# A hybrid diffusion block on one core: the sums of the later modulations as GpSimd products and additions in place of fused VectorE instructions

## The chip, the cores and the metric

The kernel runs on one core of a Trainium2 chip. The core has five engines with a queue of instructions each: TensorE (PE in the profile; PEld is its loading of weights), VectorE (DVE), ScalarE (ACT), GpSimd (POOL) and SyncE (SP). An engine takes its instructions in order; engines wait for one another by semaphores. Transfers between the memory of the chip and the core's own memory (SBUF) are issued from the queues of SyncE, ScalarE or GpSimd and done by 16 DMA engines. The metric is the device time of one execution in microseconds (us), the median of several runs.

## The reference, cut to what matters

One layer: the tokens x (256 x 2048) and a context (256 x 2048) are modulated by a condition c, pass one wide projection into three token mixers, are merged, projected and normed, and pass a squared-ReLU MLP.

```python
mod = jax.nn.silu(c) @ w_ada[l] + b_ada[l]                    # 2048 x 12288
sh1, sc1, g1, sh2, sc2, g2 = [m[:, None, :] for m in jnp.split(mod, 6, axis=-1)]
y, _ = _token_mixers(_modulate(x, sh1, sc1), lp, ctx_states, True, True)
x = _layernorm(ALPHA * x + g1 * y, ln1_g[l], ln1_b[l])
x = _layernorm(ALPHA * x + g2 * _sq_relu_mlp(_modulate(x, sh2, sc2), w_ff1[l], w_ff2[l]),
               ln2_g[l], ln2_b[l])
```

The first two modulations (sh1, sc1) are needed at once and are computed by TensorE at the start. The change concerns the product silu(c) @ w_ada for the four later ones, g1, sh2, sc2 and g2: 2048 x 8192 weights, 67 MB of float32.

## The kernel before

Every weight matrix is streamed in tiles of 512 KB (128 partitions x 1024 float32). `wload` (line 162) gets one: `wsplit` has SyncE load it into a buffer `wraw`, ScalarE casts it to a rounded part `whi` (line 138), and VectorE subtracts the two into the rest `wlo` (line 139); TensorE multiplies with both parts. There are 4 buffers with the tag `wraw`, 4 `whi` and 3 `wlo`, and 584 such tiles go through in the whole program.

The later modulations run beside that stream. `ada_parts` (line 546) is a generator; it takes 8 parts of 1024 columns, each in 16 steps. A step has one tile `aw` (128 rows of w_ada, 512 KB), multiplies each partition with its value of silu(c) (`csil`) and adds it to `acc`, in one fused instruction on VectorE, `stt` of line 564 (line 562 for the first step of a part). A step loads the tile for the next step first. At the end of a part `acc` goes to `acc_d` in the chip's memory; much later `ada_row` and `ada_cols` read it and sum over the partitions on TensorE.

`beside` (line 152) enters a generator with a rate: each `wload` moves it on by that many steps. The six first parts (g1, sh2, sc2) run at a rate of 1.0 in `dn_early` (the projections for the DeltaNet branch, 24 tiles, with the Hyena filters between them), at 0.55 in `hyena`, at 0 in `hgrn_group`, and at 0.3 in the tail of the DeltaNet branch and the branch projections (some 1060 to 1450 us). Their tiles `aw` take buffers of the tag `wraw`, the same four that the weight stream uses. The last two parts (g2) run in the MLP at 0.25 from `first_norm`, after it has scaled and shifted the residual; they have a ring of eight buffers of their own (`awr`), and there `in_turn` keeps loads and VectorE's sums in the order of the program.

Elsewhere the order on each engine is set when the program is built: a scheduler plays it through on a clock of its own and gives each instruction its place, each buffer its user, and so each wait its semaphore. `dma` (line 131) is GpSimd's queue: the program's many small transfers (filter windows, `v_d`, `g_d`, `br_d`, `acc_d`) are issued there, and little else runs on GpSimd.

Of the kernel before, what the change touches and what calls it, by code (L numbers as in the profile page):

```python
# [14 lines left out]
MUL, ADD, SUB, MAX, MIN = ALU.mult, ALU.add, ALU.subtract, ALU.max, ALU.min  # L15
# [65 lines left out]
def tile_block(ctx: ExitStack, tc: tile.TileContext, A: dict, out: bass.AP):  # L81
    nc = tc.nc
# [9 lines left out]
    def slot(shape, tag, name, dt=F32):  # L92
        uid[0] += 1
        return sbp.tile(shape, dt, name=f"{name}_{uid[0]}", tag=tag, bufs=NB[tag])
# [32 lines left out]
    ts_ = nc.vector.tensor_scalar  # L127
    stt = nc.vector.scalar_tensor_tensor
# [71 lines left out]
    csil = cst.tile([P, 2, KT], F32, name="csil")  # L200
# [112 lines left out]
    ring = slot([P, 4, 1024], "m16", "ring", F32R)  # L313
# [62 lines left out]
    for q in range(4):  # L376
        xt = page("xt", (4, 512))
        for i, src in enumerate((x_in, c_in)):
            nc.scalar.dma_start(
                out=xt[:, 2 * i:2 * i + 2, :],  # L380
                in_=src[:, q * 512:(q + 1) * 512].rearrange("(t p) c -> p t c", p=P))
        mod = slot([P, 2, 4, 2], "k1", "mod")
        for part in range(2):
            pmod = sc_ps()
            for kb in range(8):
# [3 lines left out]
                for k in range(2):  # L389
                    kt = kb * 2 + k  # L390
# [153 lines left out]
    in_turn = tc.keep_in_program_order  # L544

    def ada_parts(parts, ring=None):
        def load(b, kt):
            a = slot([P, W], "wraw", "aw") if ring is None else ring[:, (b * KT + kt) % 8]
            ld = nc.sync.dma_start(out=a, in_=w_ada[kt * P:(kt + 1) * P, 2 * D + b * W:2 * D + (b + 1) * W])
            if ring is not None:  # L550
                in_turn(ld)
            return a

        for b in parts:
            acc = slot([P, W], "k4", "acc")
            ahead = None
            for kt in range(KT):
                a = ahead if kt else load(b, kt)
                if kt < KT - 1:
                    ahead = load(b, kt + 1)  # L560
                if kt == 0:
                    op = ts_(out=acc, in0=a, scalar1=csil[:, 0, kt:kt + 1], scalar2=None, op0=MUL)
                else:
                    op = stt(out=acc, in0=a, scalar=csil[:, 0, kt:kt + 1], in1=acc, op0=MUL, op1=ADD)  # L564
                if ring is not None:
                    in_turn(op)
                if kt == KT - 1:
                    dma(out=acc_d[b], in_=acc)
                yield
# [222 lines left out]
    def dn_inverse():  # L792
# [31 lines left out]
        dma(out=dx[1], in_=M[64:P])  # L824

    beside("ada", ada_parts(range(6)), 1.0)
    dn_early()

# [641 lines left out]
    for i, pp in tm_last(ya, yb, A["w_out"][0], 0, 3 * 512, boxes):  # L1470
# [4 lines left out]
        for k4 in range(4):  # L1475
# [9 lines left out]
            for k in range(4):  # L1485
                kt = 4 * k4 + k
                if k % 2:
                    ts_(out=t[:, k, :], in0=pt[:, k * P:(k + 1) * P], scalar1=gm[:, kt:kt + 1],
                        scalar2=bm[:, kt:kt + 1], op0=MUL, op1=ADD)
# [5 lines left out]
    def first_norm():  # L1495

        for j in range(4):
            js = slice(j * 512, (j + 1) * 512)
            gr = row_bcast(A["ln1_g"][0][js], 512, "k2", "lng")
            br = row_bcast(A["ln1_b"][0][js], 512, "k2", "lnb")  # L1500
            for i in range(2):
                in_turn(tt_(out=xr[:, i, js], in0=xr[:, i, js], in1=gr, op=MUL))
                tt_(out=xr[:, i, js], in0=xr[:, i, js], in1=br, op=ADD)
                yield
        yield from ada_parts((6, 7), slot([P, 8, W], "u32", "awr"))
# [85 lines left out]
```

## Time and profile before

| | before |
|---|---|
| runs (us) | 2358.07, 2356.26, 2362.41; median 2358.07 |
| profiled execution (us) | 2355.76, of which span 2354.1 |
| TensorE busy | 2271.1 us, 96% of the span |
| VectorE busy | 1634.0 us, 69% |
| ScalarE busy | 1081.7 us, 46% |
| GpSimd busy | 181.7 us, 8% |
| moved by DMA | 511.19 MB, 217 GB/s over the span |

The profile shows one execution. Its rows give, for a group of instructions, the line of the kernel, the engine, the output and inputs by the program's names, the count, the busy time, and the idle time before them with what ended it. A row of waits says how long an engine stood still for what. A row of the windows gives the busy time of each engine in a stretch, with the granted clock of TensorE (1.00 is full) and the share of time in which the DMA engines were busy.

### The profile page before, as it was taken

The numbers are of one execution on the slowest core, as the hardware profiler recorded it, in microseconds if no ns is written. First come the engines' busy times: TensorE is split into PE (matmuls) and PEld (weight loads), VectorE is DVE, ScalarE is ACT, GpSimd is POOL, SyncE is SP. The second block draws the span as 40 slices with busy tenths as digits, with TensorE's granted clock in tenths as the row PEclk, the third lists the DMA queues.
The fourth block names the chain that finished last, engine by engine and source line by source line (L and its number), as shares of the span: only waits on it lengthen the run. The fifth ranks groups of instructions, "written<-read, shape, count | busy, mean of one in ns | idle before, by whom it ended". The sixth has DMA issues, their size and how long they took to land.

```text
span 2354.1 us, 32778 instructions
## 1 busy us (share of the span) xinstructions
PE 2271.1 (96%) x12641; PEld 1936.4 (82%) x12641; DVE 1634.0 (69%) x1972; ACT 1081.7 (46%) x1473; POOL 181.7 (8%) x293
## 2 busy tenths in 40 slices
PE   6999898999999999999999999999999999999998
PEld 4778688998888889887888877887888888888886
DVE  6776457877879999576666656666765766765667
ACT  6665434434433534644443443445544544544542
POOL 0000222000110000111030020000000000000000
PEclk9999899999999999999999999999999999999999
DMA  9958767787653323678787898664677777776664
GB/s 344 338 183 259 219 181 229 230 261 246 206 149 110 101 73 117 173 196 275 233 251 219 287 326 280 220 208 146 214 232 245 231 246 242 232 245 193 195 204 147
DMA packets 296072, 511.19 MB, mean 217 GB/s; under 512 B 17526, under 2 KB 155217, under 8 KB 293324
## 3 DMA queue, kind: packets, MB, share of 16 engines
q1 hardware_dynamic: 271488, 422.63, 56.2%
q0 software_dynamic: 21648, 82.01, 11.2%
q10 hardware_dynamic: 2780, 4.47, 0.5%
q8 instruction: 99, 1.62, 0.3%
q14 instruction: 57, 0.47, 0.1%
HBM read 474.59 MB, written 34.45 MB: 216 GB/s over the span
## 4 chain that ended last, share of the span: by engine, by line
PE 68%; DMA 7%; DVE 5%; issue 1%; ACT 1%; DVEq 0%; POOL 0%; ACTq 0%; SPq 0%
PE mm L476 10%; PE mm L519 7%; PE mm L518 7%; PE mm L520 7%; PE mm L478 5%; PE mm L846 4%; PE mm L847 3%; PE mm L845 3%; DMA aw<-in_w_ada_dram 3%; PE mm L219 3%; PE mm L218 3%; PE mm L220 3%; DVE wlo L139 2%; DMA wraw<-in_w_in_dram 2%; DMA wraw<-in_w_branch_dram 2%
## 5 line engine op out<-in xcount | busy, mean ns | idle before, releaser
L138 ACT CAST whi<-wraw 128x1024 fp32r<-128x1024 f32 x584 | 614.0, 1052 | 898.3 <-PE mm L520 226.3
L139 DVE TENSOR_TENSOR wlo<-wraw,whi 128x1024 fp32r<-128x1024 f32 x584 | 712.0, 1221 | 391.0 <-PE mm L519 127.5
L476 PE MATMUL mm<-u,whi 128*128 128x512 f32 x992 | 349.2, 397 | 0.0
L220 PE MATMUL mm<-uh,wlo 128*128 128x256 f32 (+1 forms) x1024 | 341.1, 336 | 2.9 <-DVE wlo L139 2.9
L218 PE MATMUL mm<-uh,whi 128*128 128x256 f32 (+1 forms) x960 | 319.0, 332 | 14.1 <-DVE cy L534 13.0
L219 PE MATMUL mm<-ul,whi 128*128 128x256 f32 (+1 forms) x960 | 318.9, 332 | 0.0
L478 PE MATMUL mm<-u,wlo 128*128 128x256 f32 x992 | 278.4, 281 | 0.0
L476 PEld LDWEIGHTS mm<-u,whi 128*128 128x128 f32 x992 | 186.2, 188 | 45.2
L220 PEld LDWEIGHTS mm<-uh,wlo 128*128 128x128 f32 x1024 | 198.9, 194 | 22.9 <-DVE wlo L139 3.7
L218 PEld LDWEIGHTS mm<-uh,whi 128*128 128x128 f32 x960 | 186.7, 194 | 31.7 <-issue 13.6
L219 PEld LDWEIGHTS mm<-ul,whi 128*128 128x128 f32 x960 | 186.9, 195 | 16.0 <-issue 0.7
L478 PEld LDWEIGHTS mm<-u,wlo 128*128 128x128 f32 x992 | 187.4, 189 | 0.1
L520 PE MATMUL mm<-whi,h 128*128 128x512 f32 x480 | 187.2, 390 | 0.0
L519 PE MATMUL mm<-wlo,h 128*128 128x512 f32 x480 | 186.8, 389 | 0.0
L518 PE MATMUL mm<-whi,h 128*128 128x512 f32 x480 | 186.0, 391 | 0.0
L564 DVE SCALAR_TENSOR_TENSOR acc<-aw,csil,acc 128x1024 f32<-128x1024 f32 x90 | 115.1, 1279 | 99.0 <-DMA aw<-in_w_ada_dram 98.8
L846 PE MATMUL mm<-wlo,uh 128*128 128x512 f32 x384 | 151.0, 393 | 2.4 <-DVE wlo L139 2.4
L847 PE MATMUL mm<-whi,ul 128*128 128x512 f32 x384 | 150.9, 393 | 0.0
L845 PE MATMUL mm<-whi,uh 128*128 128x512 f32 x384 | 150.5, 400 | 0.0
L518 PEld LDWEIGHTS mm<-whi,h 128*128 128x128 f32 x480 | 90.1, 188 | 19.4 <-issue 0.7
L520 PEld LDWEIGHTS mm<-whi,h 128*128 128x128 f32 x480 | 90.1, 188 | 19.0 <-issue 0.2
L519 PEld LDWEIGHTS mm<-wlo,h 128*128 128x128 f32 x480 | 90.1, 188 | 19.0 <-issue 0.5
(515 smaller groups left out, 3977.5 us busy)
## 6 DMA issues: line engine op xcount, KB each, us to landing
wraw<-in_w_in_dram SPq DMA_DIRECT2D x264, 512.0 KB, 4.1
wraw<-in_w_ff_dram SPq DMA_DIRECT2D x256, 512.0 KB, 4.0
aw<-in_w_ada_dram SPq DMA_DIRECT2D x96, 512.0 KB, 4.6
raw<-in_w_ada_dram SPq DMA_DIRECT2D x32, 1024.0 KB, 5.5
wraw<-in_w_branch_dram SPq DMA_DIRECT2D x48, 512.0 KB, 5.2
wraw<-in_w_out_dram SPq DMA_DIRECT2D x32, 512.0 KB, 4.3
awr<-in_w_ada_dram SPq DMA_DIRECT2D x32, 512.0 KB, 5.8
g_d<-gate POOLq DMA_DIRECT2D x24, 256.0 KB, 4.0
```

The costliest lines, as they stand in the source:

```text
L138: copy(out=hi, in_=src)
L139: tt_(out=lo, in0=src, in1=hi.bitcast(F32), op=SUB)
L218: mm(ps, wh[:, k, cs], ah, start=first, stop=False, skip_group_check=True)
L219: mm(ps, wh[:, k, cs], al, start=False, stop=False, skip_group_check=True)
L220: mm(ps, wl[:, k, cs], ah, start=False, stop=last, skip_group_check=True)
L476: mm(pss[ch], wh[:, k, cs], a[:, kt].rearrange("p s t -> p (s t)"), start=(kt == 0), stop=False, skip_group_check=True)
L478: mm(pss[ch][:, 0:T], wl[:, k, cs], a[:, kt, 0], start=False, stop=(kt == KT - 1), skip_group_check=True)
L518: mm(pss[i], a, wh[:, k, :], start=(kt == 0), stop=False)
L519: mm(pss[i], a, wl[:, k, :], start=False, stop=False)
L520: mm(pss[i], b, wh[:, k, :], start=False, stop=(kt == nk - 1))
L846: mm(pg[i], a, wl[:, k, :], start=False, stop=False)
L847: mm(pg[i], c, wh[:, k, :], start=False, stop=(kt == KT - 1))
```

## The change

In `ada_parts` the fused multiply-and-add leaves VectorE. On GpSimd, a step multiplies the tile in place (`aw` by `csil`) and then adds it to `acc`, two instructions; the first step of a part is one product into `acc`. The call that held the sums of the last two parts in program order is gone; that for their loads stays. The 128 steps, the loads and the rates stay.

```diff
                 if kt == 0:
-                    op = ts_(out=acc, in0=a, scalar1=csil[:, 0, kt:kt + 1], scalar2=None, op0=MUL)
+                    op = nc.gpsimd.tensor_scalar(out=acc, in0=a, scalar1=csil[:, 0, kt:kt + 1], scalar2=None, op0=MUL)
                 else:
-                    op = stt(out=acc, in0=a, scalar=csil[:, 0, kt:kt + 1], in1=acc, op0=MUL, op1=ADD)
-                if ring is not None:
-                    in_turn(op)
+                    op = nc.gpsimd.tensor_scalar(out=a, in0=a, scalar1=csil[:, 0, kt:kt + 1], scalar2=None, op0=MUL)
+                    nc.gpsimd.tensor_tensor(out=acc, in0=acc, in1=a, op=ADD)
                 if kt == KT - 1:
                     dma(out=acc_d[b], in_=acc)
```

The instructions as they are built now, at three places. In the new file lines 562 and 564 are the products and 565 the addition; numbers behind are smaller by one. First SyncE in `dn_early`, where loads of `aw` and of weight tiles take turns; what a load waits for stands in brackets, a semaphore by its owner (DVE and Pool the engines, DMAHW a transfer). Before:

```order
L549 DMA aw_1854<-in_w_ada_dram 128x1024 [waits DMAHW2_49,DVE_49]
L143 DMA wraw_1857<-in_w_in_dram 128x4x256 [waits DMAHW3_49,DVE_49]
L549 DMA aw_1887<-in_w_ada_dram 128x1024 [waits DMAHW4_49,DVE_49]
L143 DMA wraw_1890<-in_w_in_dram 128x4x256 [waits DMAHW5_49,DVE_49]
L549 DMA aw_1920<-in_w_ada_dram 128x1024 [waits DMAHW6_49,DVE_49]
L143 DMA wraw_1923<-in_w_in_dram 128x4x256 [waits DMAHW7_49,DVE_49]
```

And now:

```order
L549 DMA aw_1861<-in_w_ada_dram 128x1024 [waits DMAHW6_49,DMAHW5_49,DVE_49]
L143 DMA wraw_1865<-in_w_in_dram 128x4x256 [waits Pool_49]
L549 DMA aw_1895<-in_w_ada_dram 128x1024 [waits DMAHW7_49,DMAHW0_49,DVE_49]
L143 DMA wraw_1899<-in_w_in_dram 128x4x256 [waits Pool_49]
L549 DMA aw_1929<-in_w_ada_dram 128x1024 [waits DMAHW2_49,DMAHW1_49,DVE_49]
L143 DMA wraw_1933<-in_w_in_dram 128x4x256 [waits Pool_49]
```

The loads stand in the same order; before, each waited for VectorE to be done with a buffer, and now every weight tile here waits for an instruction of GpSimd.

Second, VectorE at the same place, where the gates of the DeltaNet branch (`gates`) are computed in a chain of small instructions. Before:

```order
L139 TENSOR_TENSOR wlo_1860<-wraw_1857,whi_1859 128x1024
L644 SCALAR_TENSOR_TENSOR gates_1279<-gates_1279 128x64
L564 SCALAR_TENSOR_TENSOR acc_1487<-aw_1887,csil,acc_1487 128x1024
L531 SCALAR_TENSOR_TENSOR cy_1627<-mm_1486,colC,cy_1627 128x4x63
L644 SCALAR_TENSOR_TENSOR gates_1279<-gates_1279 128x64
L530 SCALAR_TENSOR_TENSOR cy_1765<-mm_1632,colC,cy_1765 128x4x63
L139 TENSOR_TENSOR wlo_1893<-wraw_1890,whi_1892 128x1024
L564 SCALAR_TENSOR_TENSOR acc_1487<-aw_1920,csil,acc_1487 128x1024
L644 SCALAR_TENSOR_TENSOR gates_1279<-gates_1279 128x64
L531 SCALAR_TENSOR_TENSOR cy_1765<-mm_1632,colC,cy_1765 128x4x63
L139 TENSOR_TENSOR wlo_1926<-wraw_1923,whi_1925 128x1024
L564 SCALAR_TENSOR_TENSOR acc_1487<-aw_1953,csil,acc_1487 128x1024
```

And now:

```order
L139 TENSOR_TENSOR wlo_1598<-wraw_1595,whi_1597 128x1024
L641 TENSOR_SCALAR gates_1279<-gates_1279 128x64
L644 TENSOR_SCALAR gates_1279<-gates_1279 128x64
L643 SCALAR_TENSOR_TENSOR gates_1279<-gates_1279 128x64 x7
L645 SCALAR_TENSOR_TENSOR gates_1279<-gates_1279 128x64
L646 SCALAR_TENSOR_TENSOR gates_1279<-gates_1279 128x64
L647 SCALAR_TENSOR_TENSOR gates_1279<-gates_1279,alg_1276 128x64
L652 COPY G<-gates_1279 128x32 x2
L139 TENSOR_TENSOR wlo_1643<-wraw_1640,whi_1642 128x1024
L530 SCALAR_TENSOR_TENSOR cy_1625<-mm_1486,colC,cy_1625 128x4x63
L531 SCALAR_TENSOR_TENSOR cy_1625<-mm_1486,colC,cy_1625 128x4x63
```

The sums (line 564) stood between the links of the chain and are gone; the chain now stands together, ahead of the next weight tile's subtraction.

Third, GpSimd in `hyena`, where it had only issued transfers (to the loads of the filters' spectra, `spl`, and the stores of the gates, `g_d`). Before:

```order
L909 DMA spl_3869<-spec_90 128x2048
L300 DMA spec_93<-smdf_2973 512x1x256
L852 DMA g_d<-gate_4091 128x512
L852 DMA g_d<-gate_4094 128x512
L909 DMA spl_4131<-spec_92 128x2048
L911 DMA nyl_4133<-nyq_96 1x16x32
L568 DMA acc_d<-acc_3596 128x1024
```

And now:

```order
L564 TENSOR_SCALAR aw_3943<-aw_3943,csil 128x1024
L564 TENSOR_SCALAR aw_4012<-aw_4012,csil 128x1024
L565 TENSOR_TENSOR acc_3626<-acc_3626,aw_3943 128x1024
L564 TENSOR_SCALAR aw_4067<-aw_4067,csil 128x1024
L565 TENSOR_TENSOR acc_3626<-acc_3626,aw_4012 128x1024
L564 TENSOR_SCALAR aw_4089<-aw_4089,csil 128x1024
L565 TENSOR_TENSOR acc_3626<-acc_3626,aw_4067 128x1024
L564 TENSOR_SCALAR aw_4191<-aw_4191,csil 128x1024
L565 TENSOR_TENSOR acc_3626<-acc_3626,aw_4089 128x1024
L851 DMA g_d<-gate_4129 128x512
L910 DMA nyl_4171<-nyq_96 1x16x32
L908 DMA spl_4169<-spec_92 128x2048
L851 DMA g_d<-gate_4132 128x512
```

The products (564) and additions (565) stand between the transfers, and the addition of a step comes behind the product of the next one, which needs the next tile.

## Rows read from the trace of the kernel before

**Rows 1.** The page: span, engines, the cast behind each weight tile, two kinds of loads.

```profile
span 2354.1 us, 32778 instructions
...
PE 2271.1 (96%) x12641; PEld 1936.4 (82%) x12641; DVE 1634.0 (69%) x1972; ACT 1081.7 (46%) x1473; POOL 181.7 (8%) x293
...
L138 ACT CAST whi<-wraw 128x1024 fp32r<-128x1024 f32 x584 | 614.0, 1052 | 898.3 <-PE mm L520 226.3
...
wraw<-in_w_in_dram SPq DMA_DIRECT2D x264, 512.0 KB, 4.1
...
aw<-in_w_ada_dram SPq DMA_DIRECT2D x96, 512.0 KB, 4.6
```

**Rows 2.** Busy time of each engine in five stretches (us; instructions in brackets).

```profile
core 0: us, PE busy (x) PEld busy (x) DVE busy (x) ACT busy (x) POOL busy (x), PEclk, DMA share, GB/s
150.00:206.00 56.00, 51.79 (x313) 46.41 (x312) 45.46 (x76) 29.21 (x40) 1.16 (x3) 0.97 0.83 257
206.00:330.00 124.00, 112.41 (x568) 93.44 (x567) 61.92 (x111) 59.95 (x136) 26.50 (x41) 0.94 0.66 202
330.00:606.00 276.00, 262.14 (x1781) 242.85 (x1780) 206.63 (x266) 118.16 (x153) 30.20 (x50) 0.98 0.76 239
1060.00:1450.00 390.00, 381.63 (x1940) 314.42 (x1938) 241.42 (x265) 164.90 (x236) 54.11 (x92) 0.99 0.81 266
1753.00:2088.00 335.00, 335.00 (x1706) 284.44 (x1705) 221.34 (x225) 156.93 (x191) 0.59 (x2) 1.00 0.72 236
```

**Rows 3.** The same stretches, instructions of line 564 alone.

```profile
150.00:206.00 56.00, 16.62 (x13) 0.97 0.83 257
206.00:330.00 124.00, 15.53 (x13) 0.94 0.66 202
...
1060.00:1450.00 390.00, 37.38 (x30) 0.99 0.81 266
1753.00:2088.00 335.00, 38.35 (x30) 1.00 0.72 236
```

**Rows 4.** VectorE's groups from 330 to 606 us: busy, mean ns, idle before.

```profile
L139 DVE TENSOR_TENSOR wlo<-wraw,whi 128x1024 fp32r<-128x1024 f32 x65 | 78.7, 1213 | 15.2 <-ACT whi L138 6.4 <-issue 2.9 <-PE mm L220 2.0
L564 DVE SCALAR_TENSOR_TENSOR acc<-aw,csil,acc 128x1024 f32<-128x1024 f32 x34 | 43.4, 1277 | 30.8 <-DMA aw<-in_w_ada_dram 30.8
...
L139 DVE TENSOR_TENSOR yl<-cm,yh 128x512 fp32r<-128x512 f32 x10 | 6.7, 675 | 0.1
```

**Rows 5.** Waits from 206 to 330 us: total, times, longest (PE, then DVE).

```profile
PE mm L218 <- DVE cy L534: 5.9, 1, 5.9
PE ps L171 <- DVE ktok L605: 3.8, 1, 3.8
...
DVE acc L564 <- DMA aw<-in_w_ada_dram: 25.3, 8, 5.7
```

**Rows 6.** SyncE's issues: two of the ten loads of aw in this stretch.

```profile
171.31 0.33 SPq L549 DMA_DIRECT2D aw<-in_w_ada_dram  x1
...
205.09 0.33 SPq L549 DMA_DIRECT2D aw<-in_w_ada_dram  x1
```

**Rows 7.** The two selects of line 764 on GpSimd, and VectorE meanwhile (min/median/max ns).

```profile
641.44 1.21 DVE L139 TENSOR_TENSOR wlo<-wraw,whi 128x1024 fp32r<-128x1024 f32 x1
642.92 2.25 DVE L139 TENSOR_TENSOR yl<-cm,yh 128x512 fp32r<-128x512 f32 x1 [0.27 <-ACT yh L138]
...
L139 DVE TENSOR_TENSOR yl<-cm,yh x2: 2255/2423/2591, 642.9 to 645.1; 128x512 fp32r<-128x512 f32 x2
...
L764 POOL TENSOR_SCALAR_AFFINE_SELECT E<-E x2: 2549/3740/4932, 639.7 to 644.6; 128x2048 f32<-128x2048 f32 x2
```

**Rows 8.** Another GpSimd instruction, 1024 elements written and none read.

```profile
L1230 POOL MEMSET XT<- x4: 947/947/948, 978.8 to 1193.6; 64x1024 f32 x4
```

**Rows 9.** TensorE in a projection: three matmuls from the first row to the second.

```profile
440.01 0.28 PE L218 MATMUL mm<-uh,whi 128*128 128x256 f32 x1
...
440.38 0.28 PE L218 MATMUL mm<-uh,whi 128*128 128x256 f32 x1
```

## The prediction

> **What bounds the kernel now.** I read the page first: TensorE is busy for 2271 of 2354.1 us, VectorE for 69%, GpSimd for 8% [rows 1]. So nothing that leaves VectorE shortens the program by itself; it can only close some of TensorE's gaps, 83 us in all. Next I read the windows over the stretches in which the sums run [rows 2, 3]. From 1753 to 2088 us, the MLP with 30 of the sums, TensorE is busy throughout: there is nothing to win. The gaps lie where the sums share the four buffers `wraw` with the weight stream: TensorE is idle for 4.2 us from 150 to 206 (13 sums), 11.6 us from 206 to 330 (13), 13.9 us from 330 to 606 (34 [rows 4]) and 8.4 us from 1060 to 1450 (30). That is 38 us, the most that a perfect change could give back there, with a few more where the granted clock is under 1.00 (0.94 from 206 to 330).
>
> Then the waits: in these stretches VectorE stands before a sum because its tile has not landed, 25.3 us from 206 to 330 and 30.8 us from 330 to 606 [rows 4, 5], and what is queued behind on VectorE stands too. TensorE's largest waits from 206 to 330, 5.9 and 3.8 us, are for VectorE [rows 5]. This is the gain that the change can have.
>
> **What the change removes.** 120 fused instructions of 1.28 us, 90 of them in the four stretches [rows 3, 4], and eight first products; VectorE no longer waits for tiles `aw`. The chain of `gates` stands together. All of it lies beside TensorE's work, so it counts only through the gaps above: at most 38 us.
>
> **What it adds on GpSimd: one step.** The trace has no GpSimd arithmetic with two inputs. The nearest rows are the two selects of line 764, 2048 elements in and 2048 out, 2.55 and 4.93 us [rows 7]. They show more than a duration. The first is on record from 639.7 us, but VectorE's subtraction at 641.44 (two inputs in SBUF) runs its usual 1.21 us in it; the next one, `yl` at 642.92, takes 2.25 us where its mean is 0.675 [rows 4, 7]. It ends at 645.17, so it began 0.68 us before, some 644.5: when the first select was done (639.7 + 4.93 = 644.6). The second `yl` takes 2.59 us, and the second select 2.55. The two engines take turns, whole instruction by whole instruction; a select by itself needs about 644.6 - 642.6 = 2.0 us. A product of 1024 elements is then 1.0 us (the write-only instruction of 1024 elements took 0.947 [rows 8]). The addition reads two operands, as many elements as a select: I take 2.0 us, with 1.0 us (the second read is free) and 4.93 us (the longer select) as ends. One step is 3.0 us of GpSimd, 2.0 to 6.9, plus a turn of up to 1.2 us for each of its two instructions.
>
> [...]
>
> **Where it lies on the path.** Two things make it more than hidden work on an idle engine. First, the turns: `wlo` has two inputs in SBUF, and TensorE consumes a tile every 3 us in the narrow projections (three matmuls in 0.37 us, 24 to a tile [rows 9]). Second, the buffers: in `dn_early` SyncE's weight loads now wait for GpSimd, as the first pair of orders shows, and behind a waiting load all later loads are queued, since SyncE takes them in order; ScalarE, VectorE and TensorE wait for the tile in turn. In `hyena` an addition stands behind the next step's product, so a tile is kept until the next tile has landed.
>
> *150 to 206 us.* Ten loads of `aw` were issued 171.31 to 205.09, 3.75 us apart [rows 6]. The new loop: a weight tile lands (4.1 us), is cast (1.05) and subtracted (1.21) and frees a buffer; `aw` lands in it (4.6), its product (1.0) and the previous addition (2.0) follow, which free the buffer of the weight tile three steps on [rows 1, 4]: 14.0 us for three steps, 4.65 each. That is 0.9 us more per step, +12 us for 13 steps. With turns on each link (1.2 + 1.2 + 2.0 in three steps) it is 6.1, +30 us; with all of today's idle time gone, -4.
>
> *206 to 330 us.* 13 steps in 124 us leave time for 3.0 us each, and the 25.3 us of VectorE's waits are gone. I take -6 of TensorE's 11.6 idle us; the ends are -11.6 and, for filter windows that are issued later on GpSimd, +12.
>
> *330 to 606 us.* 34 steps, 8.1 us apart. A tile `aw` is kept for 4.6 + 8.1 + 1.0 + 2.0 = 15.7 us, before some 8 (4.6, 1.28 and about 2 in a queue, an estimate): 265 us of buffer time more, of 4 x 276 = 1104; 65 weight tiles at 6.4 us at least need 414. So 948 of 1104, 86%: prefetching becomes thin but does not run dry on average. The lock: GpSimd 34 x 3.0 = 102 us and at least 85 us of two-input work on VectorE (78.7 and 6.7 [rows 4]), 187 of 276. VectorE's own work is 206.6 - 43.4 = 163 us; with all of GpSimd's turns in front it is 265, just under the stretch. Nothing is over its limit, much is near it, so I take TensorE's idle time to grow by about three quarters: +10 us. The ends are -14 (all of it gone) and +44 (6.9 us a step: 235 + 85 = 320 of 276).
>
> *1060 to 1450 us.* 30 steps, 13 us apart, product and addition together: +4, for transfers that now queue behind them on GpSimd (the gates' loads and stores); ends -8 and +15. *1753 to 2088:* eight buffers of their own and 11 us to a step, VectorE busy for 221 of 335 us: 0, at most +5. *The clock:* about 26 us more idle time in stretches that had 0.94 to 0.98; 332 us of them at a loss of one hundredth more: +3.
>
> **The sum.** 12 - 6 + 10 + 4 + 0 + 3 = +23 us on the profiled execution's 2355.76, which makes 2379; the median of the runs is 2.3 us above it, so 2381 us. All lower ends together give 2320, all upper ones 2467. That much more than 0.3% (7 us), about what a measurement of this kernel can tell from no change.
>
> **Rivals.** *VectorE's relief wins.* If the turns cost little (additions near 1.0 us) and the waits of 25.3 and 30.8 us go, TensorE gets back most of 38 us: 2358 - 27 = 2331 us. For it speaks that TensorE's waits in [rows 5] are for VectorE. Against it: tiles that were late stay late, and the wait moves to GpSimd, with two instructions behind it and a weight load that waits for them.
>
> *It comes to nothing.* What VectorE gains is paid back in turns: 2358 us. The Trainium skill ("Perfetto Trace Analysis", Optimizing Scalar/DVE Operations) expects about this of moving work between the two engines, since they share a read port. The rows on the selects bear it out as far as the port goes.
>
> *GpSimd becomes the bound.* If an addition takes the 4.93 us of the longer select, a step is 6.9 us: 13 steps are 90 us in a stretch of 56 (+34), and 330 to 606 grows by 44, with the upper ends of the other stretches (12 + 15 + 5) some +110: 2468 us. It decides from the point where a step with its turns is longer than 4.3 us in the first stretch and 5.6 in the third ((276 - 85) / 34). Against it speaks that the 4.93 us were half waiting.
>
> That the sums do not move at all is excluded by the orders.
>
> **How the numbers follow.** The forecast (buffers and turns cost more than the relief, 2366 to 2425) has 0.50, VectorE's relief 0.20, nothing 0.17, GpSimd as the bound 0.13. Slower by over 0.3% is then 0.63, within 0.3% 0.17, faster 0.20. The range goes from 2340, into the relief, to 2425; about 0.1 lies below and 0.1 above.
>
> **What would show it.** Right: SyncE's longest new wait is a weight load for line 565; VectorE's subtractions have a mean over 1.3 us from 150 to 606; the issues of `aw` in `dn_early` are some 4.7 us apart or more; TensorE's idle time from 150 to 606 is over 40 us (now 30); the MLP is unchanged. Wrong: subtractions at 1.21 us as before (no turns), additions under 1.5 us, or TensorE with fewer waits from 150 to 606 than now. If GpSimd is busy for over 80% of 330 to 606, the last rival holds.

## The result, and the profile after

The changed kernel takes 2529.85 us (median; 2526.27 to 2537.1) against 2357.16 us beside it: a ratio of 1.0734, 95% interval 1.0714 to 1.0753, or 172.7 us more (172 below). The forecast was +23 us, the range ended at 2425. The direction was right, the size was not.

The page of the profiled execution (2533.37 us), the lines that answer to [rows 1] and to the groups of lines 139 and 564 in [rows 4]:

```profile
span 2531.7 us, 32884 instructions
...
PE 2345.0 (93%) x12641; PEld 1979.8 (78%) x12641; DVE 1663.2 (66%) x1844; ACT 1083.6 (43%) x1474; POOL 884.9 (35%) x541
...
L139 DVE TENSOR_TENSOR wlo<-wraw,whi 128x1024 fp32r<-128x1024 f32 x584 | 825.7, 1417 | 591.7 <-ACT whi L138 288.9
...
L564 POOL TENSOR_SCALAR aw<-aw,csil 128x1024 f32<-128x1024 f32 x90 | 280.3, 3114 | 272.3 <-DMA aw<-in_w_ada_dram 186.9
...
L565 POOL TENSOR_TENSOR acc<-acc,aw 128x1024 f32<-128x1024 f32 x90 | 229.2, 2546 | 2.5
```

GpSimd is busy for 885 us instead of 182. VectorE has lost 120 fused instructions and eight first products and is still busier than before (1663 against 1634 us): its subtractions of weight tiles take 1417 ns in the mean, 1221 before, 114 us together, and other instructions of VectorE are longer as well. TensorE's busy time itself has grown by 74 us for the same matmuls.

The same five stretches as in [rows 2], their borders put at the same weight tiles by counting ScalarE's casts (good to about two tiles, some 5 us; at 282 us two casts stand 12.5 us apart, so that border is good to some 10). The columns are busy us of each engine, then granted clock, share of the DMA engines and GB/s:

```profile
core 0: us, PE busy (x) PEld busy (x) DVE busy (x) ACT busy (x) POOL busy (x), PEclk, DMA share, GB/s
155.00:282.00 127.00, 92.67 (x475) 79.25 (x473) 59.98 (x104) 61.48 (x140) 85.26 (x53) 0.80 0.52 163
282.00:410.00 128.00, 114.09 (x565) 93.99 (x564) 61.59 (x76) 36.18 (x50) 89.88 (x58) 0.91 0.51 165
410.00:760.00 350.00, 284.78 (x1649) 251.26 (x1650) 206.96 (x210) 110.19 (x139) 225.13 (x106) 0.89 0.58 185
1215.00:1634.00 419.00, 394.86 (x1962) 321.11 (x1960) 257.85 (x240) 165.93 (x238) 229.53 (x157) 0.98 0.78 251
1936.00:2272.00 336.00, 336.00 (x1709) 285.03 (x1708) 219.41 (x193) 156.78 (x191) 165.86 (x61) 1.00 0.73 241
```

| stretch of before [rows 2] | before, us | after, us | difference | forecast | e17 (below) |
|---|---|---|---|---|---|
| 150 to 206, `dn_early` | 56 | 127 | +71 | +12 | +22 |
| 206 to 330 | 124 | 128 | +4 | -6 | -6 |
| 330 to 606, `hyena` | 276 | 350 | +74 | +10 | +10 |
| 1060 to 1450 | 390 | 419 | +29 | +4 | +29 |
| 1753 to 2088, MLP | 335 | 336 | +1 | 0 | +5 |

Together +179 us; the spans differ by 177.6 (e17: +60 and 60.8). In the first three, TensorE's busy time grows from 426 to 492 us and its idle time from 30 to 113. Their granted clock, 0.97, 0.94 and 0.98 before, is 0.80, 0.91 and 0.89, a mixture of its two levels (1.2 and 2.4 GHz): the growing gaps come with a lower clock, and 65 of the 149 us lost there are longer matmuls.

The durations of the two new instructions, product and addition (min/median/max ns, then first and last start in us):

```profile
L564 POOL TENSOR_SCALAR aw<-aw,csil x90: 2832/2852/4330, 155.2 to 1626.9; 128x1024 f32<-128x1024 f32 x90
```

```profile
L565 POOL TENSOR_TENSOR acc<-acc,aw x90: 2333/2403/3421, 158.6 to 1630.9; 128x1024 f32<-128x1024 f32 x90
```

This is the first thing that the prediction had wrong. The addition is near what it took (2.40 us, it said 2.0). The product is 2.85 us where it said 1.0: the instruction with one input is the *longer* of the two. A step is 5.25 us by these medians, not 3.0, and 5.66 with its turns (3114 and 2546 ns in the mean): above the first of the two points (4.3 and 5.6 us) from which the last rival, GpSimd as the bound, was to decide, and at the second. The times from one start to the next agree with these durations: of two steps without a gap, the product at 180.08 is followed by an addition at 182.90, 2.82 us later.

What that does is seen on one tile, in `dn_early`. SyncE's issues (time, duration):

```profile
183.98 0.46 SPq L549 DMA_DIRECT2D aw<-in_w_ada_dram  x1
...
196.50 0.38 SPq L143 DMA_DIRECT2D wraw<-in_w_in_dram  x1
208.44 0.33 SPq L549 DMA_DIRECT2D aw<-in_w_ada_dram  x1
208.82 0.43 SPq L143 DMA_DIRECT2D wraw<-in_w_in_dram  x1
```

and GpSimd's instructions in the same time:

```profile
189.28 3.70 POOL L564 TENSOR_SCALAR aw<-aw,csil 128x1024 f32<-128x1024 f32 x1 [3.58 <-DMA aw<-in_w_ada_dram]
197.77 0.61 POOL L681 DMA_DIRECT2D rows_d<-rT  x1 [4.79 <-ACT eT L685]
198.38 0.55 POOL L686 DMA_DIRECT2D e_d<-eT  x1
198.95 2.42 POOL L565 TENSOR_TENSOR acc<-acc,aw 128x1024 f32<-128x1024 f32 x1
201.34 2.84 POOL L564 TENSOR_SCALAR aw<-aw,csil 128x1024 f32<-128x1024 f32 x1
204.15 0.78 POOL L688 DMA_DIRECT2D inst<-rows_d  x1
204.96 2.37 POOL L565 TENSOR_TENSOR acc<-acc,aw 128x1024 f32<-128x1024 f32 x1
```

The tile loaded at 183.98 is multiplied at 189.28 and added at 204.96. In the 12 us between, GpSimd stood for 4.79 us before a transfer whose source ScalarE had not written yet, issued it and the next, and made the addition of the step before and the product of the step behind. The addition ends at 207.33; 1.1 us later, at 208.44, SyncE gets the load off that is four loads behind the one of 183.98, and with it the weight load at 208.82 that was queued behind it. Since 196.50 SyncE had issued nothing. ScalarE and TensorE get their weights later for it, and so GpSimd's transfers their sources: the loop is closed. Taken over the 13 steps of `dn_early` (k-th issue of `aw` to the end of the k-th addition), a tile is kept for 24.7 us, before for 7.3, and the issues are 9.5 us apart instead of 4.4. In `hyena` it is 18.7 us against 6.3.

### The profile page after: what moved, and what is told of

It is laid out like the page before. It is cut to its first block, busy times and chain, and to the rows that moved or that the text cites. A ratio compares the mean times of both kernels' runs of the same rounds, so it can differ in the third digit from the quotient of the medians.

```text
span 2531.7 us, 32884 instructions
## 1 busy us (share of the span) xinstructions
PE 2345.0 (93%) x12641; PEld 1979.8 (78%) x12641; DVE 1663.2 (66%) x1844; ACT 1083.6 (43%) x1474; POOL 884.9 (35%) x541
## 4 chain that ended last, share of the span: by engine, by line
PE 61%; DMA 11%; DVE 9%; issue 3%; ACT 3%; POOL 1%; SPq 0%; DVEq 0%; ACTq 0%; POOLq 0%
PE mm L476 9%; DMA wraw<-in_w_in_dram 8%; PE mm L519 7%; PE mm L520 7%; PE mm L518 7%; DVE wlo L139 5%; PE mm L478 5%; PE mm L220 3%; PE mm L219 3%; PE mm L218 3%; PE mm L845 2%; PE mm L846 2%; PE mm L844 2%; DMA wraw<-in_w_branch_dram 2%; ACT whi L138 2%
## 5 line engine op out<-in xcount | busy, mean ns | idle before, releaser
L139 DVE TENSOR_TENSOR wlo<-wraw,whi 128x1024 fp32r<-128x1024 f32 x584 | 825.7, 1417 | 591.7 <-ACT whi L138 288.9
L220 PE MATMUL mm<-uh,wlo 128*128 128x256 f32 (+1 forms) x1024 | 353.3, 350 | 37.1 <-DVE wlo L139 36.8
L564 POOL TENSOR_SCALAR aw<-aw,csil 128x1024 f32<-128x1024 f32 x90 | 280.3, 3114 | 272.3 <-DMA aw<-in_w_ada_dram 186.9
L218 PE MATMUL mm<-uh,whi 128*128 128x256 f32 (+1 forms) x960 | 333.0, 347 | 28.0 <-ACT whi L138 26.6
L219 PE MATMUL mm<-ul,whi 128*128 128x256 f32 (+1 forms) x960 | 329.3, 343 | 0.0
L218 PEld LDWEIGHTS mm<-uh,whi 128*128 128x128 f32 x960 | 197.0, 205 | 52.0 <-ACT whi L138 32.2
L565 POOL TENSOR_TENSOR acc<-acc,aw 128x1024 f32<-128x1024 f32 x90 | 229.2, 2546 | 2.5
L219 PEld LDWEIGHTS mm<-ul,whi 128*128 128x128 f32 x960 | 196.8, 205 | 16.2
L844 PE MATMUL mm<-whi,uh 128*128 128x512 f32 x384 | 153.9, 414 | 11.9 <-ACT whi L138 11.9
L564 POOL TENSOR_SCALAR awr<-awr,csil 128x1024 f32<-128x1024 f32 x30 | 96.8, 3226 | 142.4 <-DMA awr<-in_w_ada_dram 142.4
L518 PEld LDWEIGHTS mm<-whi,h 128*128 128x128 f32 x480 | 90.1, 188 | 19.4 <-issue 0.7
```

What stands on the lines that cost most here:

```text
L139: tt_(out=lo, in0=src, in1=hi.bitcast(F32), op=SUB)
L218: mm(ps, wh[:, k, cs], ah, start=first, stop=False, skip_group_check=True)
L219: mm(ps, wh[:, k, cs], al, start=False, stop=False, skip_group_check=True)
L220: mm(ps, wl[:, k, cs], ah, start=False, stop=last, skip_group_check=True)
L518: mm(pss[i], a, wh[:, k, :], start=(kt == 0), stop=False)
L564: op = nc.gpsimd.tensor_scalar(out=a, in0=a, scalar1=csil[:, 0, kt:kt + 1], scalar2=None, op0=MUL)
```

## The experiments

Differences are against the kernel before, run beside each. "Kept" is that time from load to last use, the mean of the 13 steps in `dn_early`.

### Taking the change apart: e1, e2, e14

e1 leaves both instructions on VectorE, e2 moves the addition alone, e14 has the product on ScalarE:

```diff
 e1
+op = ts_(out=a, in0=a, scalar1=csil[:, 0, kt:kt + 1], scalar2=None, op0=MUL)
+op = tt_(out=acc, in0=acc, in1=a, op=ADD)
 e2
+op = ts_(out=a, in0=a, scalar1=csil[:, 0, kt:kt + 1], scalar2=None, op0=MUL)
+nc.gpsimd.tensor_tensor(out=acc, in0=acc, in1=a, op=ADD)
 e14
+op = act(out=a, in_=a, func=AF.Copy, scale=csil[:, 0, kt:kt + 1])
+nc.gpsimd.tensor_tensor(out=acc, in0=acc, in1=a, op=ADD)
```

> Product in place and addition as in the change, but both left on VectorE: half of the change. Rate theory (a step takes GpSimd 2.85 + 2.40 = 5.3 us, longer than the pace of the loop, and all else waits for it): VectorE does a product in some 0.7 us and an addition in 1.2, against 1.28 fused, so 120 x 0.6 = 75 us more work on an engine with 30% to spare: 2357 to 2375. Port theory (GpSimd's reads block VectorE): the same, since GpSimd reads nothing. Buffer theory (any longer hold of the shared buffers costs): a tile is held 0.6 us longer, 2360 to 2390.

> The product in place on VectorE, the addition on GpSimd: the change with its mis-sized half taken back. GpSimd's step is 2.4 to 2.5 us instead of 5.3. Rate theory: 13 steps are 33 us in the 56 us of the first stretch, so most of the loss goes: 2365 to 2400. Port theory: 120 additions with two inputs still block VectorE, about half of the locked time: 2430 to 2460. Buffer theory: the tile is still kept until GpSimd has added it, behind GpSimd's transfers: 2400 to 2450.

> The change with the product on ScalarE instead of GpSimd; GpSimd adds, VectorE is free of the sums. GpSimd's step is 2.4 to 2.8 us, as in e2_addition_moved, which lost 62 us. If what counts is how long a step keeps GpSimd and so the tile: 2390 to 2430. If the product's place counts little: over 2470.

Measured: e1 2404.4 us (1.0195, 1.0166 to 1.0225; +46), e2 2419.96 (1.0255, 1.0227 to 1.0283; +62), e14 2418.72 (1.0245, 1.0220 to 1.0271; +58). Two instructions instead of one cost VectorE 752 + 1217 ns instead of 1280, as its groups in e1 say (busy us, mean ns, idle before):

```profile
L564 DVE TENSOR_SCALAR aw<-aw,csil 128x1024 f32<-128x1024 f32 x90 | 67.6, 752 | 100.4 <-DMA aw<-in_w_ada_dram 100.4
...
L565 DVE TENSOR_TENSOR acc<-acc,aw 128x1024 f32<-128x1024 f32 x90 | 109.6, 1217 | 0.9
```

e1 missed all its ranges upward, e14 came out where the length of the step had it. e2 is in the range of the buffers, 20 us above that of the step's rate, which had not priced the 46 of e1, and below the port theory, though its subtractions are nearly as slow as in the change:

```profile
L139 DVE TENSOR_TENSOR wlo<-wraw,whi 128x1024 fp32r<-128x1024 f32 x584 | 814.3, 1402 | 284.3 <-ACT whi L138 87.4
```

So slower subtractions do not by themselves come with 172 us. But the three totals are no parts of them, since they do not fall in the same places. In the MLP, where the change loses nothing, e14 loses 33 us, with TensorE idle for 20 (columns as above):

```profile
1790.00:2158.00 368.00, 348.15 (x1719) 290.58 (x1718) 215.43 (x195) 181.57 (x220) 75.17 (x34) 0.98 0.68 223
```

e1 loses 20 there (355 us from 1789 to 2144, TensorE busy for 341). That e14 hit its range is thus in part luck. In the other four stretches together, by the same count of casts, e1 loses some 36 us, e2 56, e14 35 and the change 178: the *product* on GpSimd is the larger share, the instruction that looked cheap. With the product on either other engine the tile is kept for 9.2 and 9.6 us.

### Forms of the product: e16

> For durations only: the addition is left out of parts 0 to 5, and each part has one form of product or copy on GpSimd, so the sums of parts 0 to 5 are not formed: part 0 a product of two tensors (the scalar read over and over), 1 by an immediate, 2 a tile times itself, 3 a copy, 4 by a column with 512 and with 256 elements, 5 two products in one instruction. If the slow thing is the column as scalar, 1 and 3 take 1.0 us and 0 and 2 take 2.4; if it is the one-input form itself, 1 takes 2.85 as well.

It took 2338.96 us (one run). The forms in the order of the parts (min/median/max ns):

```profile
L564 POOL TENSOR_TENSOR acc<-aw,csil x15: 1887/1894/2752, 154.2 to 216.8; 128x1024 f32<-128x1024 f32 x15
...
L566 POOL TENSOR_SCALAR acc<-aw x15: 2761/2796/4916, 234.7 to 356.9; 128x1024 f32<-128x1024 f32 x15
...
L568 POOL TENSOR_TENSOR acc<-aw x15: 1883/1894/3081, 377.7 to 487.3; 128x1024 f32<-128x1024 f32 x15
...
L570 POOL COPY acc<-aw x15: 1037/1064/4782, 505.9 to 586.7; 128x1024 f32<-128x1024 f32 x15
...
L572 POOL TENSOR_SCALAR acc<-aw,csil x15: 1560/1570/2927, 1083.3 to 1243.2; 128x512 f32<-128x512 f32 x15
...
L573 POOL TENSOR_SCALAR acc<-aw,csil x15: 912/925/2672, 1084.8 to 1244.7; 128x256 f32<-128x256 f32 x15
...
L575 POOL TENSOR_SCALAR aw<-aw,csil x15: 1109/1140/2524, 1271.2 to 1433.3; 128x1024 f32<-128x1024 f32 x15
```

Neither expectation: a copy takes 1.06 us, but an immediate is as slow as the column (2.80). A product of two tensors takes 1.89, and one instruction with *two* operations on its one input 1.14, less than half of what the same instruction takes with one. So 1.0 us was right for a pass over 1024 elements and wrong for the form that the change uses.

### The same change with the cheap form: e17

```diff
-scalar1=csil[:, 0, kt:kt + 1], scalar2=None, op0=MUL)
+scalar1=csil[:, 0, kt:kt + 1], scalar2=1.0, op0=MUL, op1=MUL)
```

> The change with the same product written with two operations, times the column and times 1.0; in e16_forms this form took 1.14 us in the median and the one-operation form 2.8. A step on GpSimd is then 3.5 us instead of 5.3, near the 3.0 that the prediction took, and below the 4.3 and 5.6 us from which it let GpSimd become the bound. (The scheduler also puts the sums of dn_early ahead of most transfers.) If the prediction's model was right but for the product's price: 2365 to 2425. If the loss follows the length of the step in a straight line through e14 (2.6 us, +58) and the change (5.6 us, +172): some 2450.

2413.73 us (1.0227, 1.0205 to 1.0249; +53), inside the range of the prediction and of its model with the price put right. Its five stretches:

```profile
155.00:233.00 78.00, 62.94 (x347) 56.94 (x345) 52.70 (x71) 37.30 (x80) 52.14 (x31) 0.87 0.58 185
233.00:351.00 118.00, 110.69 (x550) 91.21 (x551) 60.84 (x85) 49.96 (x94) 80.35 (x68) 0.96 0.70 216
351.00:637.00 286.00, 264.19 (x1761) 241.71 (x1759) 196.68 (x230) 116.26 (x151) 181.38 (x118) 0.97 0.73 230
1093.00:1512.00 419.00, 394.38 (x1954) 324.26 (x1953) 242.52 (x239) 164.42 (x237) 179.15 (x155) 0.97 0.76 249
1816.00:2156.00 340.00, 340.00 (x1727) 288.30 (x1726) 233.01 (x196) 158.44 (x193) 122.02 (x61) 1.00 0.74 242
```

They are the last column of the table above: +22, -6, +10, +29, +5 against a forecast of +12, -6, +10, +4, 0. A tile is kept for 10.5 us. The straight line (2450) is out. Within the range it is still more than twice the +23 of the forecast. What the run cannot part is length and order: with the shorter product the scheduler also put the sums of `dn_early` ahead of most transfers.

### Order on GpSimd alone: e3, e5, e6

e3 lets no product be queued ahead of the addition before it. e5 is the kernel before with the stores of ScalarE's results on ScalarE's own queue, e6 is e3 with these:

```diff
 e3
+with tc.issue_after(done.ins):
+    mul(a)
+done = nc.gpsimd.tensor_tensor(out=acc, in0=acc, in1=a, op=ADD)
 e5, e6
-dma(out=kc_d, in_=kch)
+put(out=kc_d, in_=kch)
```

> The change, but the product of a step may not be queued on GpSimd before the addition of the step before it, so no tile is kept for the landing of the next one. Order theory (the loss in hyena comes from tiles kept for a step longer): about half of the 85 us lost there comes back, 2480 to 2500. Rate and port theory: the same instructions of the same length, 2520 to 2540.

> The kernel before, with those stores of dn_early, hyena and the gates whose source ScalarE writes (rT, eT, kkq, kch, qch, kxq, vt, ny, gate, bth) issued on ScalarE's queue instead of GpSimd's. The reference for the next run. Both theories: 2350 to 2375, since nothing of the sums changes.

> The change in pairs (no product ahead of the addition before it) and these same stores on ScalarE's queue, so that little that waits for other engines stands between a product and its addition. Queue theory (a tile is kept because its addition is queued on GpSimd behind transfers and products that wait for work that itself waits for weights; in the change 24.7 us from load to addition in dn_early, 7.3 before): the tile is kept for 10 to 13 us and most of the 172 us comes back, 2385 to 2440. Duration theory (the product's 2.85 us and the port are what costs, whatever the order): instructions and durations stay, 2480 to 2520.

e3 2517.62 us (1.0663, 1.0635 to 1.0690), e5 2364.72 (1.0026, 1.0013 to 1.0040), e6 2487.47 (1.0552, 1.0523 to 1.0580). Tiles are kept for 23.0 and 16.9 us in e3 and e6. Order by itself is worth 13 and, with the stores away, 44 of the 172 us; e3 is between its two expectations, e6 inside that of the durations. At 5.25 us a step, better order does not rescue it: `inst`, a load that waits for one of those stores, still stood 11.9 us between a product and its addition in e6.

### Keeping the tiles: e4, e7, e9, e10, e11

```diff
 e4, e7
+for k, t in [late] * (late is not None) + [(kt, a)] * (kt == KT - 1 or ring is not None):
...
+    op = stt(out=acc, in0=t, scalar=csil[:, 0, k:k + 1], in1=acc, op0=MUL, op1=ADD)
+    in_turn(op)
+late = (kt, a) if ring is None else None
 e9, e10, e11
-"k8": 7,
+"k8": 6, "aws": 2,
-a = slot([P, W], "wraw", "aw")
+a = slot([P, W], "aws", "aw")
 e11
-ld = nc.sync.dma_start(
+ld = nc.gpsimd.dma_start(
```

(e4 has no `in_turn` there.)

> The kernel before, fused on VectorE, but each fused instruction of parts 0 to 5 is issued one step later, so that three of the four shared buffers can be with the sums, as in the change; GpSimd does no arithmetic. Buffer theory: a loss like that of the change in the shared stretches, 2420 to 2520. Rate and port theory: VectorE's work is the same and nothing is slower, 2355 to 2375.

> As e4_hold, but each late fused instruction is pinned behind what VectorE has in the program before it, since in e4_hold the scheduler put it back to where it was (a tile was kept for 7.2 us as before). Buffer theory (keeping three of the four shared buffers is enough to lose time, whoever does it): a tile is kept for 10 to 16 us, and 2400 to 2500. Queue and port theory: VectorE waits for nothing that waits for it, at most 2380.

> The kernel before, sums fused on VectorE, but the tiles aw of parts 0 to 5 have two buffers of their own instead of sharing the four of wraw; the space is one of the seven 8 KB pages (k8 6). The reference for the next two runs. Both theories: 2340 to 2375.

> The change with these two buffers of its own; loads of aw still issued by SyncE. Circle theory (GpSimd's late additions keep shared buffers, so weight loads stop, so the work that GpSimd's own transfers wait for stops): the four weight buffers stay free, but a load of aw that waits for its buffer still stands ahead of weight loads in SyncE's order, so part of the loss goes, 2400 to 2470. Port theory (GpSimd's reads slow VectorE down): the same instructions, 2490 to 2540.

> The change with two buffers of its own and its loads issued by GpSimd itself, so that neither a buffer nor a queue ties the weights to the sums (the scheduler then also lets the sums begin earlier). Circle theory: nothing is left to close it, 2340 to 2390. Port theory: GpSimd reads and writes as much beside VectorE, 2480 to 2540.

e4, 2358.06 us (0.9990, 0.9977 to 1.0002), says nothing: the scheduler moved the late instruction back and the tiles were kept for 7.2 us. e7, pinned, takes 2709.53 us (1.1489, 1.1454 to 1.1524): a tile is kept for 38.7 us, far longer than meant, and the program loses twice what the change loses, though GpSimd does no arithmetic and the subtractions have their 1.23 us. Uses of a shared tile that stand late in an engine's queue are enough to stop the weights.

With two buffers of their own (and six 8 KB pages instead of seven) the sums on VectorE take 2399.18 us (e9, 1.0155, 1.0121 to 1.0190; 24 more than expected), the change 2457.52 (e10, 1.0404, 1.0361 to 1.0447): 58 us between them, where it was 172 with shared buffers. Where these 58 lie says more. The two stretches of e10 that answer to 150 to 606 and 606 to 1060 us before (456 and 454 us):

```profile
195.00:647.00 452.00, 427.79 (x2662) 384.99 (x2661) 304.92 (x389) 210.99 (x335) 330.78 (x184) 0.96 0.68 215
647.00:1168.00 521.00, 467.94 (x3072) 411.07 (x3072) 450.13 (x460) 200.30 (x279) 226.73 (x110) 0.95 0.51 149
```

In the first, with 47 of the steps, GpSimd's products and additions are as long as in the change (3.49 and 2.59 us in the mean), VectorE's subtractions slow (1.52 us), and nothing is lost, where the change took 605 us with 60 steps. So neither the length of the step nor the slower subtractions cost the change its 149 us there by themselves; what e10 lacks is the sharing of the buffers. The loss of e10 is in the second stretch (521 us, in e9 457). The reservation: the scheduler begins these sums at once, so they end at 917 us in e10 (9.5 us to a step) and at 420 in e9, and the start that answers to the first 150 us before takes 195 and 182. e11, loads on GpSimd's queue too, is not better, 2462.89 us (1.0428, 1.0394 to 1.0462), against the theory's 2340 to 2390. Its loss is in that second stretch too (552 us), a stage in which TensorE waits for VectorE's small work, as this wait (total, times, longest) shows:

```profile
PE ps L1046 <- DVE Qt L1065: 24.0, 9, 5.1
```

### GpSimd's arithmetic alone: e8, e12, e13, e18, e15

The sums stay off GpSimd, which works beside them on a tile that nobody reads. e8 was timed by the tile itself, the others by a column that ScalarE copies out of it; e18 also relieves VectorE:

```diff
 e13, e18
+copy(out=tick, in_=a[:, 0:1])
+for t in (tick, csil[:, 0, kt:kt + 1]):
+    nc.gpsimd.tensor_tensor(out=dum, in0=bc(t, [P, W]), in1=bc(csil[:, 0, 0:1], [P, W]), op=ADD, saturate=False)
 e18
-op = stt(out=acc, in0=a, scalar=csil[:, 0, kt:kt + 1], in1=acc, op0=MUL, op1=ADD)
+op = act(out=acc, in_=a, func=AF.Copy, scale=csil[:, 0, kt:kt + 1])
```

> The kernel before, with its sums fused on VectorE; beside each sum of parts 0 to 5 GpSimd runs three in-place products and three additions of 320 elements on a tile of its own that nobody reads. The first product reads one column of the tile of the sum, so that it is timed by its landing. GpSimd's arithmetic is about that of the change, but no shared buffer waits for an addition. Port theory: the subtractions get slower as in the change (1.42 us in the mean instead of 1.22) and so does the program, 2430 to 2530. Queue theory: subtractions slower by as much, but hidden, 2360 to 2400.

> As e8_port, where GpSimd's idle work turned out too long (7.5 us a step) and held the tile that it was timed by. Now a step is three products and two additions of 220 elements, timed by a column that ScalarE copies out of the tile, so GpSimd can be late without holding anything of the sums. Port theory: VectorE stands behind GpSimd as in the change, 2450 to 2530. Circle theory: some transfers on GpSimd are later, 2360 to 2410.

> As e12_port_free (GpSimd works beside the sums and holds nothing), but with two additions of 1024 elements to a step, as long as those of the change; in e12 the instructions were short and the subtractions hardly slower (1.24 us). The operands are columns read over and over, the output is one byte an element into a tile that nobody reads. Port theory: subtractions of 1.4 us in the mean, and a good part of the 172 us, 2450 to 2530. Circle theory: the same slower subtractions and 2365 to 2425, most of it in hyena, where VectorE has the least room.

> As e13_port_long (two additions of 1024 elements to a step on GpSimd that hold nothing), but VectorE is relieved of the sums of parts 0 to 5 as in the change: ScalarE writes each product to acc and nothing is added, so those sums are not formed. Port theory (a step of 5 us on GpSimd costs by itself, beside a relieved VectorE): 2430 to 2500. Circle theory (it costs because tiles wait for it): 2335 to 2380; e16, where the additions were left out and GpSimd had 1 to 3 us to a step, took 2339.

> Only parts 6 and 7 as in the change (in the MLP, in the ring of eight buffers of their own), parts 0 to 5 fused on VectorE. Subtractions in the MLP as slow as in the change. Both theories, by the change's own trace: nothing is lost there, 2355 to 2365. If slower subtractions by themselves cost: 2370 to 2400.

e8 (2552.12 us, 1.0819, 1.0785 to 1.0853) is no test: its idle work kept the tiles. e12 takes 2395.24 us (1.0140, 1.0094 to 1.0186), but its short instructions left the subtractions at 1.24 us. e13 takes 2506.95 (1.0619, 1.0599 to 1.0640; +147), as the port theory wanted. VectorE from 150 to 640 us in it:

```profile
L139 DVE TENSOR_TENSOR wlo<-wraw,whi 128x1024 fp32r<-128x1024 f32 x76 | 130.2, 1718 | 21.0 <-PE mm L220 10.2 <-issue 6.0 <-ACT whi L138 3.5
L573 DVE SCALAR_TENSOR_TENSOR acc<-aw,csil,acc 128x1024 f32<-128x1024 f32 x50 | 95.6, 1912 | 42.7 <-DMA aw<-in_w_ada_dram 42.6
```

There VectorE also does the sums, and they wait as the subtractions do (1912 ns, 1277 before); so in `dn_early` a tile is kept for 10.8 us, by VectorE. With the sums gone, as in the change, e18 takes 2395.58 us (1.0147, 1.0126 to 1.0169; +35), with a step of 4.5 us in the mean on GpSimd, somewhat shorter than the change's 5.66 (busy us, mean ns):

```profile
L570 POOL TENSOR_TENSOR dum<-csil 128x1024 fp8e4<-128x1024 f32 x96 | 219.0, 2282 | 5.4
L570 POOL TENSOR_TENSOR dum<-ticks,csil 128x1024 fp8e4<-128x1024 f32 x96 | 213.5, 2224 | 188.9 <-ACT ticks L567 186.6
```

and subtractions from 150 to 640 us that are slower than the change's in the stretch that answers to it (150 to 775, its line behind):

```profile
L139 DVE TENSOR_TENSOR wlo<-wraw,whi 128x1024 fp32r<-128x1024 f32 x95 | 174.1, 1840 | 48.2 <-PE mm L220 22.2 <-ACT whi L138 18.7 <-ACT junk L605 5.2
```

```profile
L139 DVE TENSOR_TENSOR wlo<-wraw,whi 128x1024 fp32r<-128x1024 f32 x96 | 161.3, 1684 | 180.3 <-ACT whi L138 180.0
```

So GpSimd's arithmetic by itself, beside a relieved VectorE and with no tile kept by it, costs some 35 us here, between the two expectations. (ScalarE's products are in it.) The same arithmetic costs 147 where VectorE has its own two-input sums to do.

e15, only the MLP's sums on GpSimd, takes 2358.75 us (0.9995, 0.9982 to 1.0007). The change's own MLP shows why, subtractions from 1936 to 2272 us:

```profile
L139 DVE TENSOR_TENSOR wlo<-wraw,whi 128x1024 fp32r<-128x1024 f32 x121 | 182.2, 1506 | 99.3 <-PE mm L519 54.7 <-PE mm L478 19.8 <-issue 16.0
```

They are slower here too, but TensorE is busy for 336.00 of the 336 us (its window above).

## Why the prediction was wrong

**The first step that failed is the price of the product**, "a product of 1024 elements is then 1.0 us", taken from half a select and a memset. It is 2.85 us in the change. That row was near for another form: 1.06 us for a copy, 1.14 for two operations (e16). With that form in place, the change takes 2414 us, and the second and third stretch come out at -6 and +10, as forecast (e17). Some 120 of the 172 us thus hang on how the product is written, with the order that the scheduler makes of it.

**The second is the loop that the price was put into.** With 2.85 and 2.40 us, the prediction's own sum for 150 to 206 gives 16.25 us for three steps, 5.4 each, +22 us (+41 with its turns), and measured were +71; for 330 to 606 it gives buffers used to 93% (34 x 17.95 + 414 of 1104) and a lock of 264 of 276 us, still nothing over its limit, and measured were +74. What it left out is that a tile waits on GpSimd's queue behind transfers that wait for work that waits for weights: 24.7 us in `dn_early`. Without the shared buffers a step of the same instructions cost nothing in these stretches (e10).

**The rival that came nearest** was GpSimd as the bound, with a chance of 0.13; its 2468 us was still 62 short, and that it came so near is luck: it rests on an addition of 4.93 us that took 2.40. It had the long step right, but it counted GpSimd's work only, and in e10 a step as long loses nothing from `dn_early` to `hyena`. Its sign, "GpSimd busy for over 80%" in the third stretch, did not come: it is 225 of 350 us, 64%, since GpSimd itself waits in the loop for tiles and transfers. Busy shares do not show such a bound; the keeping of tiles shows the loop (24.7 us in `dn_early`, three times the 7.3 of before; the prediction had 15.7 us for `hyena`, it was 18.7).

**The terms.** 150 to 206: +71 instead of +12. The orders showed transfers between products and additions on GpSimd, the sum had none. With the short product it is still +22. 206 to 330: +4 in the change is no sign, its border being good to 10 us; -6 in e17, as forecast. 330 to 606: +74, beyond the upper end of +44. 1060 to 1450: +29, beyond the upper end of +15, and the same +29 in e17, so it does not come from the product's length; what it is was not settled. There 30 additions stand beside subtractions of 1.5 us. The MLP: +1, as said. The clock: 3 us were given to it; TensorE's busy time in the first three stretches alone grew by 65. The turns: each of GpSimd's two instructions was given one; the trace shows it for the addition, hardly for the product (last section).

**What it said would show.** Subtractions over 1.3 us, issues of `aw` over 4.7 us apart (9.5), TensorE idle for more than 40 us (113), the MLP unchanged: all there. SyncE's longest wait of the new kind is a weight load for line 562, the ones for 565 stay below 6 us (total, times, longest):

```profile
SPq L143 <- POOL acc L565: 37.2, 13, 5.8
...
SPq L143 <- POOL acc L562: 24.9, 5, 12.9
```

Most of what SyncE waits for is thus booked on others; the loop had to be read from one tile's times.

**What the 172 us are, as far as shown:** some 35 for GpSimd's arithmetic beside VectorE (e18), and most of the rest for shared buffers that GpSimd keeps for too long: of the 149 lost in the first three stretches none is left with buffers of their own (e10). Order on GpSimd's queue is 13 to 44 (e3, e6). The +29 from 1060 to 1450 are open. The relief of VectorE, half of the change's sense, shows only where GpSimd has no addition in the first six parts: e16, one run with these sums left unformed, is the only one clearly below the kernel before. No complete version here beats it; e15 equals it.

## What to carry to other kernels

Price an instruction on another engine by the same *form* there, not by its elements: look for a row with the same operations and operands, and if there is none let the range reach the point where that engine can no longer keep pace. Before moving the last use of a buffer to another queue, write down what stands ahead of that use in the queue and what those instructions wait for; if that leads back to the buffer, the loss is far larger than the work moved. And where two engines slow each other down, ask whether the slowed one has anything to give: in the MLP the same edit was free.

## What the hardware showed that was not expected

On GpSimd, one operation on one input of 1024 elements takes 2.80 to 2.85 us with a column or an immediate, 1.57 with 512 and 0.93 with 256 elements, and two operations in one instruction take 1.14. An addition of two tiles takes 2.40, of a tile with itself (a product in e16) 1.89.

VectorE's instructions do not all wait. From 1060 to 1450 us before and in the same stretch after (1215 to 1634), groups of VectorE with their mean ns:

```profile
L1330 DVE TENSOR_TENSOR vs<-ps,ex 128x512 f32<-128x512 f32 x12 | 8.3, 689 | 7.1 <-DMA g_d<-gate 3.7 <-ACT vn L1327 2.2 <-PE ps L1323 1.1
...
L1317 DVE TENSOR_TENSOR R<-R,vkk 128x512 f32<-128x512 f32 x12 | 8.1, 687 | 0.2
```

```profile
L1316 DVE TENSOR_TENSOR R<-R,vkk 128x512 f32<-128x512 f32 x12 | 11.5, 968 | 0.2
...
L1329 DVE TENSOR_TENSOR vs<-ps,ex 128x512 f32<-128x512 f32 x12 | 8.2, 685 | 4.1 <-ACT vn L1326 3.3 <-PE ps L1322 0.7
```

With one operand from TensorE's results, `vs` keeps its time (689 and 685 ns); with two in SBUF, `R` goes from 687 to 968. The gates' small instructions, 128x64 with one SBUF input, wait as well when one meets GpSimd's addition (182 and 186 ns before, with two of them here). The subtraction between them (`wlo`) starts while a product runs, whose row stands behind, and does not wait:

```profile
178.23 3.00 DVE L637 TENSOR_SCALAR gates<-gates 128x64 f32<-128x64 f32 x1 [2.12 <-ACT gates L635]
...
182.26 1.22 DVE L139 TENSOR_TENSOR wlo<-wraw,whi 128x1024 fp32r<-128x1024 f32 x1
183.40 2.36 DVE L641 TENSOR_SCALAR gates<-gates 128x64 f32<-128x64 f32 x1
```

```profile
180.08 2.83 POOL L564 TENSOR_SCALAR aw<-aw,csil 128x1024 f32<-128x1024 f32 x1
```

Nor does every instruction of GpSimd hold VectorE up. In the whole trace after, 74 weight subtractions start while an addition of GpSimd runs, and one of them takes under 1.3 us; 73 start while a product runs, and 56 do. In e17, with two operations in the product, it is 8 of 38. So nearly all of what slows the subtractions here is the addition, and the shorter product is the one that blocks more.

The Trainium skill ("SBUF — State Buffer", Who interferes with whom) says of this that two-input instructions contend with GpSimd's reads, and that the gates' form can too, in a mode that uses both ports. For the additions these rows agree, 2.36 and 3.00 us instead of 0.19; the product reads SBUF as well, and there the measurement decides: most subtractions pass.
